# DeltaNet outputs produced channel-major by swapped matmul operands, with norms from VectorE block transposes

## The chip, the core and the metric

The kernel runs on one core of a Trainium2 chip. The metric is device microseconds of one execution. The engines are PE (TensorE, matmul and its weight loads), DVE (VectorE), ACT (ScalarE), POOL (GpSimd) and SP (SyncE, which here only issues DMAs). Each engine works through its own instructions in a fixed order, and an instruction that waits holds everything behind it on that engine.

## The reference

One hybrid layer: the normalised input goes through one projection; its columns feed three token mixers, DeltaNet (6 heads of 128), GLA (5) and forgetting attention (5); their outputs are gated, put side by side and go through one output projection. There are 512 tokens and 16 meta tokens ahead of them; the width is 2048. The part that the change touches is DeltaNet's output, its norm and its gate:

```python
def gated_head_norm(o, z, w):
    o = o * lax.rsqrt(jnp.mean(o * o, axis=-1, keepdims=True) + EPS) * w
    return o.reshape(z.shape) * jax.nn.silu(z)
...
    def step(s, inp):
        qk_c, qd, kd, u_c, w_c, gl = inp
        v_new = u_c - jnp.einsum('bhck,bhkv->bhcv', w_c, s)
        o = jnp.einsum('bhck,bhkv->bhcv', qd, s) + jnp.einsum('bhcs,bhsv->bhcv', qk_c, v_new)
        s = s * gl[..., None, None] + jnp.einsum('bhck,bhcv->bhkv', kd, v_new)
        return s, o
```

For each head and token the 128 channels of `o` are divided by their root mean square, multiplied by the channel's weight `w` and by the gate `silu(z)`. Queries are normalised to unit length first; the kernel folds that factor into the same norm.

## The kernel before

**The stream of weights.** Most of the time goes to the input and output projections. Each float32 weight block of 128x1024 is loaded (`raw`, by SP, L144), split into a rounded high part (`whi`, ACT, L167) and the rest (`wlo`, DVE, L168), and multiplied in three products with the split activations (`xh`, `xl`), in the matmuls of L242, into PSUM tiles `pp`. Evacuations (L363, L392) and the convolutions with SiLU (L612, L614 on DVE, L374 on POOL, L375 to L377 on ACT, L378 on DVE) follow each block. The mixers are put in between: their small matmuls stand between the big ones on PE, and their elementwise work between the splits on DVE, ACT and POOL. The program is written in the order of its parts; a scheduler that simulates a timeline then fixes each engine's order, with some places given by hand (`place`, `soon`, `late`, which name a position in the list of big matmuls). So an edit can move instructions that it doesn't name.

**DeltaNet** runs in two groups, g = 0 and 1, of three heads (H = 3). For each group `dn_keys` builds, over four blocks of 128 tokens and the meta block, the key transposes `pk` (PE, L679), decay tiles `e` (DVE L717, ACT L718, POOL L719), the scaled keys `kd` (L693), column factors `cols` (L704 to L709) and the products `an` (L723); `dn_values` transposes the values (`vp`); `dn_queries` the queries (`qT`); `dn_inverse` sends `an` through DRAM (the stores `scr`, the load `ab`, issued by ACT) and inverts its 32x32 blocks in a loop of 60 DVE instructions (L749, L753). The preparation of group 1 stands beside the mixing of group 0.

**`dn_mix`** goes over the four blocks b. Per block: `pks` and `py` (PE), `y` (ACT), the state step `psn`, the scores `pa` of the next block and its decayed queries `eg` (SP load from DRAM L924, ACT L925, POOL L928), and the output `po`: for each head two accumulating 128x128 matmuls (L971, L972). In `po` tokens lie on the partitions and channels along the row. ACT squares each head with a running sum (L975), four small instructions on DVE and ACT make the factor of each token, and ACT writes the scaled `on` (L984). One block later `gated` transposes `on` by PE (L902, tile `pt`) and DVE multiplies it with the channel weight `dnws` and the gate, in place in the gate's tile `zsdz` (L905), which is channel-major. After the group, SP stores the three `zsdz` to DRAM (`zd`, L1362).

**The query norms** (`query_sums`) take the sum of squares of `qT` over channels, which lie on partitions there: DVE transposes 32x32 blocks (L885), POOL squares (L888), DVE sums pieces (L889), and one matmul with the constant `fold` (L891) adds the pieces across partition quarters. `fold` is made from the identity by two DVE instructions (L832, L833) inside the tile `vpm`, in `dn_values`.

**Buffers.** Tag `t15` (128x384) has six buffers that all the three-head tiles share; `qs` (the workspace of the query norms) has one; PSUM tag `m` holds the mixers' PSUM tiles.

## Time and profile before

| what | value |
|---|---|
| time, median of 3 runs | 967.24 us (965.45 to 969.41) |
| the profiled execution | 966.72 us |
| its span, first to last instruction | 964.8 us |
| granted clock of TensorE, mean | 0.999 |
| busy: DVE, ACT, POOL | 688.2, 474.5, 233.0 us |
| output transposes L902 on PE | x24, 4.6 us busy |
| scalings L905 on DVE | x24, 6.9 us busy |
| squares L975 and scaled copies L984 on ACT | x24 each, 6.3 and 7.0 us busy |
| the blocks of group 0, group 1 | first `po` 251.8 us; last L905 477.3 us |

Read the span as PE's: all other engines have idle time, and what they do costs something only where PE waits for it. Matmul durations overlap, since matmuls are pipelined, so differences between starts tell the real price of one. The lines on which the prediction rests are shown in it.

### The profile page before, as it was taken

The numbers are of one execution on the slowest core, as the hardware profiler recorded it, in microseconds if no ns is written. First come the engines' busy times: TensorE is split into PE (matmuls) and PEld (weight loads), VectorE is DVE, ScalarE is ACT, GpSimd is POOL, SyncE is SP. The second block draws the span as 40 slices with busy tenths as digits, with TensorE's granted clock in tenths as the row PEclk, the third lists the DMA queues.
The fourth block names the chain that finished last, engine by engine and source line by source line (L and its number), as shares of the span: only waits on it lengthen the run. The fifth ranks groups of instructions, "written<-read, shape, count | busy, mean of one in ns | idle before, by whom it ended". The sixth has DMA issues, their size and how long they took to land.

```text
span 964.8 us, 18868 instructions
## 1 busy us (share of the span) xinstructions
PE 955.4 (99%) x7271; PEld 882.4 (91%) x7271; DVE 688.2 (71%) x1491; ACT 474.5 (49%) x1004; POOL 233.0 (24%) x262
## 2 busy tenths in 40 slices
...
GB/s 355 298 136 209 180 205 212 287 227 227 171 167 221 226 233 192 188 119 83 186 133 179 158 185 180 187 216 225 190 210 175 181 285 281 131 218 217 178 128 175
DMA packets 70334, 191.86 MB, mean 199 GB/s; under 512 B 14077, under 2 KB 17325, under 8 KB 69476
## 3 DMA queue, kind: packets, MB, share of 16 engines
...
q14 instruction: 33, 0.27, 0.1%
...
## 4 chain that ended last, share of the span: by engine, by line
PE 97%; DVE 1%; DMA 1%; ACT 0%; issue 0%; POOL 0%; ACTq 0%; SPq 0%; DVEq 0%; POOLq 0%
PE pp L242 48%; PE pp_a L569 8%; PE pq L1452 6%; PE pp L321 5%; PE pa L1452 3%; PE pt L1452 3%; PE ps L1452 3%; PE pp_b L569 2%; PE pp_c L569 2%; PE pp_d L569 2%; PE pr L1452 1%; PE pss L1087 1%; PE pfo L1328 1%; PE pfa L1279 1%; PE pgate L415 1%; PE pg L716 1%
## 5 line engine op out<-in xcount | busy, mean ns | idle before, releaser
L242 PE MATMUL pp<-xh,whi 128*128 128x264 f32 (+2 forms) x1120 | 269.6, 305 | 0.0
L242 PE MATMUL pp<-xl,whi 128*128 128x264 f32 (+2 forms) x1120 | 269.6, 305 | 0.0
L242 PE MATMUL pp<-xh,wlo 128*128 128x264 f32 (+2 forms) x1120 | 268.4, 305 | 0.2 <-DVE wlo L168 0.2
L167 ACT CAST whi<-raw 128x1024 fp32r<-128x1024 f32 x131 | 137.2, 1047 | 158.8 <-PE pp L242 97.3
L168 DVE TENSOR_TENSOR wlo<-raw,whi 128x1024 fp32r<-128x1024 f32 x131 | 165.0, 1260 | 62.6 <-ACT whi L167 59.9
L242 PEld LDWEIGHTS pp<-xh,whi 128*128 128x128 f32 x1120 | 181.2, 188 | 8.9 <-issue 0.3
L242 PEld LDWEIGHTS pp<-xl,whi 128*128 128x128 f32 x1120 | 181.5, 189 | 8.4
L242 PEld LDWEIGHTS pp<-xh,wlo 128*128 128x128 f32 x1120 | 181.1, 189 | 8.8 <-DVE wlo L168 0.5
L374 POOL TENSOR_SCALAR stc<-cv 128x528 f32<-128x528 f32 (+1 forms) x18 | 29.0, 1614 | 104.1 <-DVE cv L614 88.1
L614 DVE SCALAR_TENSOR_TENSOR cv<-pb,cpk,cv 128x528 f32<-128x528 f32 (+1 forms) x54 | 40.8, 756 | 0.6
L168 DVE TENSOR_TENSOR wlos<-raws,whis 128x1024 fp32r<-128x1024 f32 x20 | 24.2, 1222 | 14.6 <-ACT whis L167 14.6
L167 ACT CAST whis<-raws 128x1024 fp32r<-128x1024 f32 x20 | 20.7, 1049 | 26.8 <-PE pq L1452 12.5
L321 PE MATMUL pp<-xh,wf 128*128 128x512 f32 x128 | 33.1, 398 | 0.0
L1481 POOL TENSOR_TENSOR acc<-acc,fw 128x512 f32<-128x512 f32 x4 | 6.1, 1544 | 107.9 <-DVE wll L168 107.9
L569 PE MATMUL pp_a<-t,whi 128*128 128x264 f32 (+1 forms) x224 | 29.7, 282 | 0.0
L321 PEld LDWEIGHTS pp<-xh,wf 128*128 128x128 f32 x128 | 24.2, 190 | 5.6
L569 PE MATMUL pp_a<-xl,whi 128*128 128x264 f32 x112 | 28.5, 287 | 0.0
L569 PE MATMUL pp_a<-xh,whi 128*128 128x264 f32 x112 | 28.4, 286 | 0.0
L569 PEld LDWEIGHTS pp_a<-t,whi 128*128 128x128 f32 x224 | 27.8, 188 | 0.1
L363 DVE TENSOR_TENSOR pb<-pp,rstd 128x264 f32<-128x264 f32 (+1 forms) x36 | 13.8, 424 | 18.1 <-PE pp L242 18.0
L374 POOL TENSOR_SCALAR stdz<-zdz 128x512 f32<-128x512 f32 x6 | 11.2, 1874 | 62.5 <-DMA ti<-in_w_in 50.0
L481 POOL DMA_DIRECT2D tw<-tw x16 | 13.4, 835 | 51.7 <-DVE wlo L168 25.3
...
## 6 DMA issues: line engine op xcount, KB each, us to landing
raw<-in_w_in SPq DMA_DIRECT2D x103, 512.0 KB, 3.9
ti<-in_w_in SPq DMA_DIRECT2D x28, 512.0 KB, 5.2
raw<-ti SPq DMA_DIRECT2D x28, 512.0 KB, 3.5
tw<-in_w_dn SPq DMA_DIRECT2D x20, 512.0 KB, 5.3
raws<-tw SPq DMA_DIRECT2D x15, 512.0 KB, 4.0
ti<-in_w_in POOLq DMA_DIRECT2D x14, 512.0 KB, 6.3
ti<-ti POOLq DMA_DIRECT2D x14, 512.0 KB, 6.3
tw<-in_w_dn POOLq DMA_DIRECT2D x10, 512.0 KB, 6.6
```

What stands on the lines that cost most here:

```text
L167: pace[0] = A.copy(hi, raw).ins
L168: pace[1] = V.tensor_tensor(out=lo, in0=raw, in1=hi.bitcast(F32), op=ALU.subtract).ins
L242: mm = PE.matmul(p_[:, :nt], wt[:, j * m : (j + 1) * m], xx[k][:, t0 : t0 + nt], start=(k == 0 and wt is hi and xx is xh), stop=(k == KT - ...
L321: PE.matmul(begun[i][0][0][:, :S], wt[:, i * P : (i + 1) * P], xx[k][:, NM:T], start=k + n == 0, stop=k == KT - 1 and n == 2)
L363: V.tensor_tensor(out=o, in0=p_[rows], in1=rstd[rows, t0 : t0 + n], op=ALU.mult)
L374: maxes.append(G.tensor_scalar_max(t, src, LOW).ins)
L415: PE.matmul(pgate[a][:, :HT], wg[k // 8][:, k % 8, :], xx[k][:, a * HT : (a + 1) * HT], start=(k == 0 and xx is xh), stop=(k == KT - 1 and ...
L481: x = G.dma_start(out=out_[s], in_=in_[s], accum_op=ALU.add, max_dma_last_dim=2048)
L569: m = PE.matmul(p_[:, cols], wt[:, j * P : (j + 1) * P], xx[j][part_][:, cols], start=first and i == 0, stop=i == len(todo) - 1, skip_grou ...
L614: V.scalar_tensor_tensor(out=c, in0=pb[:, t0 + w : w + T], scalar=cwc[:, blk, w : w + 1], in1=c, op0=ALU.mult, op1=ALU.add)
L716: PE.matmul(pg[:r, j * r : (j + 1) * r], kT[:, j, ts], kT[:, j, ts], start=True, stop=True)
L1452: mm = PE.matmul(p_, o_[:, s], w_, start=(first and n == 0), stop=(last and n == 2), skip_group_check=True)
```

## The change

The two output matmuls of each head swap their operands: `y` and `sst` are now the loaded ones, `at` and `eg` stream, so `po` comes out with channels on partitions, as `zsdz` has them. The 24 transposes and the scalings behind them, the 24 squares, the four small factor instructions of each block and the 24 scaled copies go. Per block DVE now transposes the 32x32 blocks of `po` into `ot` (L989), multiplies `po` by the channel weight and the gate into `zsdz` (L991), ACT squares `ot` (L993) and DVE sums pieces of 32 (L994) into a part of the `qs` tile. After the last block of the group `normed` folds the pieces by one matmul (`pqo`, L903), makes the factor of all blocks at once (L908 to L911), transposes it (`pf`, L913), copies it to `ft` (L915), stores it to DRAM by four small DMAs (`fd`, L918), loads it back broadcast to all 128 partitions (`fb`, L921, 128x1536), and POOL multiplies the three `zsdz` by it (L923). `fb` has the tag `qs`, with its one buffer. `fold` is now made in the `qs` tile too (L881, L882), at the start of `query_sums`. The tile `vpm` is smaller.

```diff
--- before.py
+++ after.py
@@ -824,14 +824,10 @@
 
     def dn_values(g, st):
         vp = six.tile([P, NN, P], F32, tag="six", name=f"vp{g}")
-        vpm3 = t15(f"vpm{g}")
+        vpm3 = t15(f"vpm{g}", (P, 2, P))
         vpm = vpm3[:, 0]
         vms = vpm3[:, 1]
         G.memset(vms, 0.0)
-        fold = vpm3[:, 2].rearrange("p (i a) -> p i a", i=4)
-        V.reduce_sum(fold[:, 0], ident.rearrange("p (i a) -> p a i", a=32), axis=mybir.AxisListType.X)
-        V.tensor_copy(fold[:, 1:], fold[:, 0].unsqueeze(1).to_broadcast([P, 3, 32]))
-        st["fold"] = vpm3[:, 2]
         br = st["br"]
         brm = st["brm"]
         G.memset(brm, 0.0)
@@ -874,12 +870,17 @@
         sq_ = wk.tile([P, NB, H], F32, tag="sqq", name=f"sqq{g}")
         so_ = wk.tile([P, NB, H], F32, tag="soo", name=f"soo{g}")
         f_ = wk.tile([P, 2, NB, H], F32, tag="ff", name=f"ff{g}")
-        egs, egls, ons = {}, {}, {}
+        egs, egls = {}, {}
+        zt = triples["dz", g]
 
         def query_sums():
 
             qs = wk.tile([P, 2 * T + 2 * S], F32, tag="qs", bufs=1, name=f"qs{g}")
-            sums = qs[:, H * S : H * S + 16 * H].rearrange("p (h m) -> p h m", h=H)
+            sums, st["sums"], st["fold"] = (qs[:, H * S + a : H * S + b] for a, b in ((0, 16 * H), (16 * H, 32 * H), (32 * H, 32 * H + P)))
+            f4 = st["fold"].rearrange("p (i a) -> p i a", i=4)
+            V.reduce_sum(f4[:, 0], ident.rearrange("p (i a) -> p a i", a=32), axis=mybir.AxisListType.X)
+            V.tensor_copy(f4[:, 1:], f4[:, 0].unsqueeze(1).to_broadcast([P, 3, 32]))
+            sums = sums.rearrange("p (h m) -> p h m", h=H)
             for j in range(H):
                 t = qs[:, j * S : j * S + S]
                 x = V.transpose(t, qT[:, j, NM:])
@@ -896,14 +897,30 @@
             A.activation(f_[:, 0], sq_, AF.Ln, bias=eps_c)
             A.activation(f_[:, 1], f_[:, 0], AF.Exp, scale=-1.0)
 
-        def gated(b):
-            pt = psm.tile([P, 512], F32, tag="m", name=f"pt{g}{b}")
+        def normed():
+
+            pq = psm.tile([P, 512], F32, tag="m", name=f"pqo{g}")
+            PE.matmul(pq[:, : 16 * H], st["fold"], st["sums"], start=True, stop=True)
+            for i in range(4):
+                r = slice(32 * i, 32 * i + 32)
+                A.copy(so_[r], pq[r, : 16 * H].rearrange("p (b h i) -> p b h i", h=H, i=4)[:, :, :, i])
+            f1, f2 = f_[:, 0], f_[:, 1]
+            V.tensor_tensor(out=f2, in0=f2, in1=so_, op=ALU.mult)
+            A.activation(f2, f2, AF.Ln, scale=1.0 / (P * P), bias=eps_c)
+            V.tensor_tensor(out=f1, in0=f1, in1=f2, op=ALU.add)
+            A.activation(f1, f1, AF.Exp, scale=-0.5)
+            pf = psm.tile([P, 512], F32, tag="m", name=f"pf{g}")
+            PE.transpose(pf[: NB * H, :P], f1.rearrange("p b h -> p (b h)"), ident)
+            ft = t15(f"ft{g}", (NB * H, P))
+            A.copy(ft, pf[: NB * H, :P])
+            fd = drp.tile([H, NB, P], F32, name=f"fd{g}")
+            for b in range(NB):
+                nc.sync.dma_start(out=fd[:, b], in_=ft[b * H : b * H + H])
+            fb = wk.tile([P, 2 * T + 2 * S], F32, tag="qs", bufs=1, name=f"fb{g}")[:, : H * S]
+            fb = fb.rearrange("p (h t) -> p h t", h=H)
+            nc.sync.dma_start(out=fb, in_=fd.rearrange("h b t -> h (b t)").partition_broadcast(P))
             for j in range(H):
-                PE.transpose(pt[:, j * P : (j + 1) * P], ons[b][:, j, :], ident)
-            for j in range(H):
-                o = zs["dz", H * g + j][:, b * P : (b + 1) * P]
-                V.scalar_tensor_tensor(out=o, in0=pt[:, j * P : (j + 1) * P], scalar=dnws[:, 0:1], in1=o,
-                                       op0=ALU.mult, op1=ALU.mult)
+                G.tensor_tensor(out=zt[:, j, :S], in0=zt[:, j, :S], in1=fb[:, j], op=ALU.mult)
 
         def soon(mm, b, i):
             if g == 1:
@@ -963,29 +980,22 @@
                     V.scalar_tensor_tensor(out=sn[:, j, :], in0=sst[:, j, :], scalar=egl[:, j : j + 1],
                                            in1=pn[:, j * P : (j + 1) * P], op0=ALU.mult, op1=ALU.add)
                 scores(b + 1)
-            if b:
-                gated(b - 1)
             po = psm.tile([P, 512], F32, tag="m", name=f"po{g}{b}")
             for j in range(H):
                 pj = po[:, j * P : (j + 1) * P]
-                PE.matmul(pj, at[:, b * H + j, :], y[:, j, :], start=True, stop=False)
-                PE.matmul(pj, eg[:, j, :], sst[:, j, :], start=False, stop=True)
-            for j in range(H):
-                sq = wk.tile([P, P], BF16, tag="sq", name=f"sqo{g}{b}{j}")
-                A.activation(sq, po[:, j * P : (j + 1) * P], AF.Square, accum_out=so_[:, b, j : j + 1])
-
-            f1, f2 = f_[:, 0, b, :], f_[:, 1, b, :]
-            V.tensor_tensor(out=f2, in0=f2, in1=so_[:, b, :], op=ALU.mult)
-            A.activation(f2, f2, AF.Ln, scale=1.0 / (P * P), bias=eps_c)
-            V.tensor_tensor(out=f1, in0=f1, in1=f2, op=ALU.add)
-            A.activation(f1, f1, AF.Exp, scale=-0.5)
-            on = t15(f"on{g}{b}")
-            for j in range(H):
-                A.activation(on[:, j, :], po[:, j * P : (j + 1) * P], AF.Copy, scale=f1[:, j : j + 1])
-            ons[b] = on
+                PE.matmul(pj, y[:, j, :], at[:, b * H + j, :], start=True, stop=False)
+                PE.matmul(pj, sst[:, j, :], eg[:, j, :], start=False, stop=True)
+            ot = t15(f"ot{g}{b}")
+            V.transpose(ot.rearrange("p h t -> p (h t)"), po[:, : H * P])
+            zb = zt[:, :, b * P : (b + 1) * P]
+            V.scalar_tensor_tensor(out=zb, in0=po[:, : H * P].rearrange("p (h t) -> p h t", h=H), scalar=dnws[:, 0:1],
+                                   in1=zb, op0=ALU.mult, op1=ALU.mult)
+            A.activation(ot, ot, AF.Square)
+            V.reduce_sum(st["sums"][:, 4 * H * b : 4 * H * (b + 1)], ot.rearrange("p h (i c) -> p (h i) c", c=32),
+                         axis=mybir.AxisListType.X)
             if b < NB - 1:
                 sst = sn
-        gated(NB - 1)
+        normed()
 
 
     def tok_values(parts, name, v, t512, t16):
```

In the changed program line numbers lie 4 lower behind `dn_values` and 10 higher behind `dn_mix` (the stores `zd` are L1372).

**PE, the end of group 0.** In these rows `pp22_0` and `pp22_1` are the two halves of one projected block, `pt03` the last output transposes of group 0, `pk14`, `pk10`, `pk11` key transposes of group 1. Before (the last of three `pt03`, which alternate with `pk14`, and what follows):

```order
L902 MATMUL pt03_2492<-ident_79,on03_2488 128x128
L679 MATMUL pk14_3044<-ident_79,kT1_2647 16x128
L679 MATMUL pk10_3061<-ident_79,kT1_2647 128x128 x3
L679 MATMUL pk11_3079<-ident_79,kT1_2647 128x128 x3
L242 MATMUL pp22_1_3773<-xl5_241,whi22_0_3777 128x258
L242 MATMUL pp22_0_3772<-xh5_240,wlo22_0_3778 128x258
```

and now, around the first small matmuls behind group 0's last block:

```order
L242 MATMUL pp22_0_3730<-xl7_285,whi22_0_3735 128x258
L913 MATMUL pf0_2445<-ident_79,ff0_2242 12x128
L679 MATMUL pk14_3004<-ident_79,kT1_2607 16x128 x3
L679 MATMUL pk10_3021<-ident_79,kT1_2607 128x128 x3
L679 MATMUL pk11_3039<-ident_79,kT1_2607 128x128 x3
L242 MATMUL pp22_1_3731<-xl7_285,whi22_0_3735 128x258
```

The transposes `pt03` are gone, the factor's transpose `pf0` stands in their stead, 12 big matmuls (L242) further back, and the key transposes of group 1 have moved behind it.

**SP, the stores at the end of group 0.** `raw24_0` to `raw25_0` are weight blocks of the input projection, `tw` rows of a table copied by the way. Before:

```order
L144 DMA raw23_1_3957<-in_w_in 128x1024
L146 DMA tw_670<-in_w_dn 16x8192
L1362 DMA zd_671<-zsdz0_527 128x512 x3
L144 DMA raw24_0_4484<-in_w_in 128x1024
L146 DMA tw_670<-in_w_dn 16x8192
L144 DMA raw24_1_4515<-in_w_in 128x1024
```

and now:

```order
L144 DMA raw23_1_3915<-in_w_in 128x1024
L146 DMA tw_670<-in_w_dn 16x8192
L918 DMA fd0_2449<-ft0_2447 3x128 x4
L921 DMA fb0_2454<-fd0_2449 128x1536
L144 DMA raw24_0_4404<-in_w_in 128x1024
L146 DMA tw_670<-in_w_dn 16x8192
L1372 DMA zd_671<-zsdz0_527 128x512 x2
L144 DMA raw24_1_4435<-in_w_in 128x1024
L146 DMA tw_670<-in_w_dn 16x8192
L1372 DMA zd_671<-zsdz0_527 128x512
L144 DMA raw25_0_4477<-in_w_in 128x1024
```

The stores of the factor and its broadcast load stand ahead of `raw24_0`; the three stores of the outputs have moved behind `raw24_0` and are parted by `raw24_1`.

**DVE, the preparation of group 1.** `cv4` is a convolution, `cols1`, `an1` and `anm1` belong to `dn_keys` of group 1, `vpm1` and `qs1` are the tiles in which `fold` was and is made. Before, some dozen rows behind the last products of `cv4` (L614):

```order
L709 TENSOR_TENSOR cols1_3042<-cols1_3042 128x12
L709 TENSOR_TENSOR cols1_3042<-cols1_3042 16x3
L723 SCALAR_TENSOR_TENSOR anm1_3040<-pg14_3149,cols1_3042,e214_3150 16x16 x3
L723 SCALAR_TENSOR_TENSOR an1_3036<-pg10_3162,cols1_3042,e210_3163 128x128 x3
L723 SCALAR_TENSOR_TENSOR an1_3036<-pg11_3175,cols1_3042,e211_3176 128x128 x3
L723 SCALAR_TENSOR_TENSOR an1_3036<-pg12_3188,cols1_3042,e212_3189 128x128 x3
L832 TENSOR_REDUCE vpm1_3215<-ident_79 128x32
L839 COPY cols1_3042<-cols1_3042 16x1
L168 TENSOR_TENSOR wlo24_0_4488<-raw24_0_4484,whi24_0_4487 128x1024
L833 COPY vpm1_3215<-vpm1_3215 128x96
L723 SCALAR_TENSOR_TENSOR an1_3036<-pg13_3201,cols1_3042,e213_3202 128x128 x3
```

and now:

```order
L693 TENSOR_SCALAR kd1_2994<-pk12_3057,at1_2995 128x128 x3
L693 TENSOR_SCALAR kd1_2994<-pk13_3075,at1_2995 128x128 x3
L704 TENSOR_TENSOR cols1_3002<-cols1_3002 128x12
L704 TENSOR_TENSOR cols1_3002<-cols1_3002 16x3
L614 SCALAR_TENSOR_TENSOR cv4_3845<-pb4_3729,cpk_90,cv4_3845 128x512
L881 TENSOR_REDUCE qs1_4209<-ident_79 128x32
L705 SCALAR_TENSOR_TENSOR cols1_3002<-cols1_3002 128x12
L705 SCALAR_TENSOR_TENSOR cols1_3002<-cols1_3002 16x3
L614 SCALAR_TENSOR_TENSOR cv4_3845<-pb4_3729,cpk_90,cv4_3845 128x512
L882 COPY qs1_4209<-qs1_4209 128x96
L706 COPY cols1_3002<-cols1_3002 128x12
L706 COPY cols1_3002<-cols1_3002 16x3
```

The reduction that makes `fold` stood behind the third triple of products `an1`; now it stands ahead of the column factors (L705), between the last two products of `cv4`, with its copy three instructions further. Its tile is the next user of the one `qs` buffer after `fb0`, so it waits for the broadcast's landing and for the last of POOL's three products.

## The prediction

> **What bounds the kernel now.** I read the busy times first, then the chain of work that ended last, then the table of waits of PE, then the windows around the place where the change inserts new work.
>
> ```profile
> PE 955.4 (99%) x7271; PEld 882.4 (91%) x7271; DVE 688.2 (71%) x1491; ACT 474.5 (49%) x1004; POOL 233.0 (24%) x262
> ...
> PE 97%; DVE 1%; DMA 1%; ACT 0%; issue 0%; POOL 0%; ACTq 0%; SPq 0%; DVEq 0%; POOLq 0%
> ```
>
> ```profile
> PE warm L310 <- POOL ones L115: 1.2, 1, 1.2
> PE pp L242 <- DVE wlo L168: 0.2, 1, 0.2
> PE pp_b L569 <- ACT whi L167: 0.2, 1, 0.2
> ```
>
> PE is the bound all the way: it is busy for 99% of the span, the chain runs through it for 97%, and its three waits sum to 1.6 us, 1.2 of them at the start. Two rules follow. An instruction taken from PE is worth its issue spacing at once, wherever it stands. Work taken from DVE and ACT is worth nothing by itself, but a wait that is put on them can starve PE, whose weights they split (whi L167 on ACT, wlo L168 on DVE). So I ask where DVE has no room.
>
> ```profile
> 305.00:372.00 67.00, 67.00 (x379) 58.10 (x378) 58.54 (x148) 23.47 (x45) 23.20 (x24) 1.00 0.83 223
> 372.00:520.00 148.00, 148.00 (x1434) 139.65 (x1433) 84.63 (x195) 62.53 (x148) 35.94 (x42) 1.00 0.58 148
> ```
>
> In these rows the columns are length, PE, PEld, DVE, ACT, POOL busy, then clock, DMA share and GB/s. From 305 to 372 us DVE is busy 58.5 of 67 us (87%): this is where the second group's inverse is built, just behind the end of the first group. Behind the second group DVE is busy 84.6 of 148 us (57%). The first place is the one to fear.
>
> **PE: removed and added.**
>
> ```profile
> 266.79 0.49 PE L902 MATMUL pt<-ident,on 128*128 128x128 f32 x3
> 267.12 0.39 PE L971 MATMUL po<-y,at 128*128 128x128 f32 x2
> ```
>
> ```profile
> 247.41 0.32 PE L891 MATMUL pq<-qs,vpm 128*128 128x48 f32 x2
> 247.55 0.49 PE L242 MATMUL pp<-xh,wlo 128*128 128x264 f32 x2
> ```
>
> The durations overlap, so I take differences of starts. Three output transposes take 267.12 − 266.79 = 0.33 us, 0.11 each; 24 go: −2.64 us. Added per group are one 48-column fold matmul, at most 0.14 (247.55 − 247.41, there two with nothing between), and one transpose, 0.11: 2 × 0.25 = +0.50. Net −2.14 us, −1.07 for each group. The output matmuls swap which operand is loaded and which streams; count and shape stay. I cost that at 0: in the rows above one more 128x128 matmul adds 0.10 to 0.11 (0.49 for three, 0.39 for two) whether it is pt or po.
>
> **DVE and ACT inside the blocks.**
>
> ```profile
> L905 DVE SCALAR_TENSOR_TENSOR zsdz<-pt,dnws,zsdz x24: 329/343/351, 267.6 to 477.3; 128x128 f32<-128x128 f32 x24
> ...
> L922 DVE TENSOR_TENSOR at<-pa,at x8: 549/550/557, 241.6 to 454.6; 128x384 f32<-128x384 f32 x8
> ...
> L885 DVE STREAM_TRANSPOSE qs<-qT x6: 668/670/711, 215.2 to 386.5; 128x512 f32<-128x512 f32 x6
> ...
> L889 DVE TENSOR_REDUCE qs<-qs x6: 670/672/675, 218.3 to 392.1; 128x16 f32<-128x512 f32 x6
> ...
> L978 DVE TENSOR_TENSOR ff<-ff,soo x8: 158/164/564, 257.3 to 471.1; 128x3 f32<-128x3 f32 x8
> ...
> L925 ACT ACTIVATE eg<-eg x8: 508/524/530, 241.9 to 454.1; 128x384 f32<-128x384 f32 x8
> ```
>
> Per block DVE loses 3 × 0.343 + 2 × 0.164 = 1.36 us. It gains a block transpose of 384 elements, 0.67 × 384/512 = 0.50; a product of the size of L922, 0.55; a reduction of 384, 0.50: 1.55. That is +0.19 a block, 1.5 us in all, hidden behind PE as the 13% and 43% idle allow. ACT loses three squares with their accumulator reads, two small steps and three scaled copies a block and gains one square of the size of L925, 0.52: it is relieved. In place of the scalings, the gate product now waits only for `po`, not for the norm. Nothing of this is on PE's path, unless the block's next step stands behind it; the rivals price that.
>
> **The new chain at the end of a group.** In the changed order the factor's transpose pf0 comes 12 big matmuls past the old place of the last output transposes, with the key transposes L679 behind it.
>
> ```profile
> 300.87 0.37 PE L242 MATMUL pp<-xl,whi 128*128 128x258 f32 x1
> ...
> 302.29 0.40 PE L242 MATMUL pp<-xl,whi 128*128 128x258 f32 x2
> ```
>
> ```profile
> 301.36 1.30 SPq L1362 DMA_DIRECT2D zd<-zsdz  x3
> ```
>
> ```profile
> gb<-gd ACTq DMA_DIRECT2D x2, 792.0 KB, 6.2
> ...
> zd<-zsdz SPq DMA_DIRECT2D x6, 256.0 KB, 7.4
> ...
> fqk<-gd ACTq DMA_DIRECT2D x5, 264.0 KB, 3.7
> ...
> scmeta<-anm ACTq DMA_DIRECT2D x2, 3.0 KB, 2.0
> ```
>
> ```profile
> L1481 POOL TENSOR_TENSOR accs<-accs,fw x8: 1292/1310/1331, 939.7 to 948.4; 128x512 f32<-128x512 f32 x8
> ...
> L1111 POOL TENSOR_TENSOR gt<-gt,gqk x3: 1808/2458/3248, 490.6 to 599.4; 128x512 f32<-128x512 f32 x2, 64x512 f32<-64x512 f32 x1
> ```
>
> Twelve matmuls past 300.87 is 302.29; less the twelve small matmuls of that block that are now gone or behind (12 × 0.11 = 1.32) and nine earlier output transposes (0.99), plus the fold (0.14): pf0 at 300.1. With 0.27 for its passage (its spacing of 0.11 and the 0.16 by which a run of three, 0.49, outlasts its 0.33) and an ACT copy, put at 0.5 like L925's 384 elements, ft0 stands at 300.9. SP then issues four small stores fd; three issues took 1.30 us, so four take 1.7: 302.6. Their landing: 2.0 us (a 3 KB store, scmeta) to 7.4 (zd<-zsdz, the larger stores from the same place); I take 3, near the small one, as these move 1.5 KB each: 305.6. The broadcast fb (768 KB to 128 partitions) then lands 6.2 us after its issue, by gb<-gd of 792 KB in the same form; its own issue 0.4: 305.6 + 0.4 + 6.2 = 312.2; bounds 3.7 (fqk<-gd, a third of the bytes) and 7.4. Three POOL products of 128x512: 1.31 each alone, 2.46 where crowded. I take 1.35: POOL ends at **316.3**. All low ends together give 302.6 + 2.0 + 0.4 + 3.7 + 3.9 = 312.6, all high ends 325.2.
>
> Hidden or not?
>
> The outputs go to DRAM behind it and are read back only for the output projection, so they themselves have time. Three engines' queues carry the wait, though.
>
> ```profile
> 305.85 1.53 DVE L168 TENSOR_TENSOR wlo<-raw,whi 128x1024 fp32r<-128x1024 f32 x1
> ...
> 326.65 1.21 DVE L168 TENSOR_TENSOR wlo<-raw,whi 128x1024 fp32r<-128x1024 f32 x1
> ```
>
> ```profile
> 312.58 0.34 SPq L144 DMA_DIRECT2D raw<-in_w_in  x1
> ```
>
> ```profile
> raw<-in_w_in SPq DMA_DIRECT2D x103, 512.0 KB, 3.9
> ```
>
> SP: between raw24_0 and raw24_1 (312.58) now stand two of the stores zd<-zsdz, which need POOL's products; raw24_1 moves to about 315.2 and lands at 319, while its split wlo24_1 stood at 326.65: covered by 7 us. DVE, ACT and POOL: the decay tile e213 takes over the slot of ft0, so it waits for fd's landing (305.6); it stands behind wlo23_0 (305.85 to 307.4): covered by 1.8 us, and beyond that any excess waits ahead of the next place, not on top of it. The third is a buffer. The fold matrix, made on DVE in L832 of before in a tile of its own, is now made in the `qs` tile (L881), whose tag has one buffer, and fb uses the same tag. So **DVE waits at L881 of the second group until POOL's third product is done**, and all of DVE's work queues behind: the column operations L705 to L709, wlo, and the products `an` L723, which the store scr of ACT awaits.
>
> ```profile
> 313.96 0.23 DVE L705 SCALAR_TENSOR_TENSOR cols<-cols 128x12 f32<-128x12 f32 x2
> ...
> 320.64 0.86 DVE L723 SCALAR_TENSOR_TENSOR an<-pg,cols,e 128x128 f32<-128x128 f32 x3
> ...
> 307.31 2.41 DVE L693 TENSOR_SCALAR kd<-pk,at 128x128 f32<-128x128 f32 x9
> ```
>
> ```profile
> 333.50 0.20 DVE L749 TENSOR_TENSOR ab<-ab 51x30 f32<-51x30 f32 x1 [0.43 <-DMA ab<-scr]
> ...
> 337.17 0.69 DVE L378 TENSOR_TENSOR qT<-cv,stc 128x512 f32<-128x512 f32 x1 [1.51 <-ACT stc L377]
> ...
> 338.28 0.68 DVE L392 TENSOR_TENSOR zgz<-pp,rstd 128x512 f32<-128x512 f32 x1
> ...
> 345.42 1.21 DVE L168 TENSOR_TENSOR wlo<-raw,whi 128x1024 fp32r<-128x1024 f32 x1
> ...
> 356.73 1.21 DVE L168 TENSOR_TENSOR wlo<-raw,whi 128x1024 fp32r<-128x1024 f32 x1
> ```
>
> ```profile
> 347.91 0.40 PE L242 MATMUL pp<-xh,wlo 128*128 128x512 f32 x1
> ```
>
> ```profile
> 359.00 0.40 PE L242 MATMUL pp<-xh,wlo 128*128 128x512 f32 x1
> ```
>
> DVE would come to L881 at 313.96 plus six `kd` that now stand later (2.41/9 = 0.27 each, 1.6), less 0.4 for what the removed scalings free: about 315.2. It waits 316.3 − 315.2 = 1.1 us. From there to the last `an` stands the same work as from 313.96 to 321.50 before, 7.5 us: `an` ends at 323.8 instead of 321.5, so the inverse, which starts when scr and ab have gone through DRAM, starts 2.3 us later (1.2 without the wait). Up to the evacuation of zgz0 (338.28) one L614 of 0.66 moves in, while the qT product and the idle 1.51 ahead of it (2.1 together) move out: +0.85. From there the weight split of 345.42 (wlo26_0) ends at 346.63 and PE first uses it at 347.91 (its place in the order of PE's matmuls counted off): slack 1.28. PE now arrives 1.07 earlier, so the slack is 0.21, and the delay 0.85, or 1.45 if the qT product finds no idle time: a stall of 0.64 to 1.24. For the next but one (wlo27_0, from 356.73 to 357.94, used at 359.00, slack 1.06) it is 0.2 more. I take **1.2 us**; it grows one for one with the end of POOL, and it does not fall to nothing without the wait, but to some 0.2. Group 0 nets −1.07 + 1.2 = +0.1.
>
> Group 1: the same chain, but nobody reuses `qs` behind it, and DVE has the room shown above. PE loses 1.07. Two of GLA's score steps, 24 big matmuls apart before, now stand together; what prepares the later one had 24 × 0.12 = 2.9 us between them. Between 0 and 0.5 I charge 0.3: −0.8.
>
> **Sum:** 966.72 us of the profiled execution (964.8 span, 1.9 around it) + 0.1 − 0.8 = 966.0. The median of the runs shown is 0.5 higher, so on that footing **966.5 us**. A measurement of this kernel can tell about 0.5%, 4.8 us, from no change: this is no change.
>
> The Trainium skill (SBUF — State Buffer, "Who interferes with whom") says that a DVE instruction with two SBUF inputs and a GpSimd one that reads SBUF exclude each other for the whole instruction. L1481 beside L1111 (1.31 against 2.46 us for 128x512) agrees that neighbours matter. By it, POOL's products would be cheap in group 0 just because DVE waits at L881; were DVE still busy, the sum above would take the 2.46.
>
> **Rivals.**
>
> *No wait (A).* If fd takes 2.0 and fb 4.5 us (between the 3.7 and the 6.2), POOL ends at 302.6 + 2.0 + 0.4 + 4.5 + 4.0 = 313.5, ahead of DVE. The stall falls to 0.2, the sum to 966.72 − 2.14 + 0.2 + 0.3 = 965.1, 965.6 on the median. For it: fqk's 264 KB land in 3.7. Against it: gb's 6.2 is the nearest in size and form.
>
> The Trainium skill (DMA: Bandwidth & Descriptors, "Anatomy of one DMA — SWDGE (gpsimd) path") gives about 2.0 us fixed and 436 GB/s, an estimate of 3.8 us for 768 KB. By this rule rival A holds; gb<-gd at 6.2 speaks against it.
>
> *DVE held long (B, slower).* One mechanism: both DMAs in series land as late as zd<-zsdz does at this place, 7.4 each, and the products run at 2.46. POOL ends at 302.6 + 7.4 + 0.4 + 7.4 + 7.4 = 325.2, 8.9 later; the stall grows by as much: 966.5 + 8.9 = 975.4. It decides from POOL's end at 316.3 + 4.8 + 0.7 = 321.8 on. For it: DMA share 0.83 in this window, the highest. Against: fd is tiny, and DVE idles at the time.
>
> *The blocks pay (C).* The transposes are gone, but block transposes and reductions now stand in DVE's queue ahead of the state steps; if each block holds PE up for the added transpose, 0.50 × 8 = 4.0 us: 970.5.
>
> **How the numbers follow.** Forecast 0.58, A 0.20, B 0.14, C 0.08. The forecast's own range is 964.5 to 969. The range for 8 in 10 takes in A less the scatter of the runs (the lowest lies 1.8 below the median) and C with the near part of B: 963.8 to 971.2. Faster by over 0.5% needs 962.4, more than the whole saving on PE: 0.03. Slower by over 0.5% is most of B and a tail of C: 0.14. The same: 0.83.
>
> **What would show it.** PE's matmul starts: no L902, pqo and pf at 0.11 to 0.14. DVE idle ahead of L881 of group 1, released by POOL, about 1.1 us (A: none; B: over 6). PE waits on wlo near 345 to 360 us, about 1.2 (B: up to 10). fb's landing 6.2 after its issue, fd's 3. Block reductions at 0.5 with no PE wait on `py` or `psn` (C: 0.5 in each). The forecast is wrong if PE waits at another place, or if group 1 waits as well.

## The result and the profile after

| | before | after |
|---|---|---|
| median | 966.53 us, 6 runs (965.45 to 969.41) | 974.25 us, 4 runs (973.36 to 976.9) |
| profiled execution | 966.72 us | 976.9 us |
| its span | 964.8 us | 975.2 us |
| ratio after/before | | 1.0082, interval 1.0058 to 1.0105 |

The change is slower by 0.8%, 7.7 us; forecast was no change. Two further executions of the changed kernel, of 1566 and 2415 us, were disturbed and are left out. The profiled execution of after lies 2.6 us above the median of its four.

The page's busy times and its chain of work that ended last, after:

```profile
PE 957.5 (98%) x7253; PEld 882.7 (91%) x7253; DVE 698.3 (72%) x1479; ACT 464.6 (48%) x938; POOL 239.1 (25%) x268
...
PE 82%; DMA 5%; DVE 5%; issue 3%; ACT 2%; POOL 1%; ACTq 0%; SPq 0%; POOLq 0%; DVEq 0%
```

PE's table of waits, after (us in total, times, longest):

```profile
PE pss L1097 <- DVE kq L1077: 3.0, 3, 1.6
PE pp_a L569 <- ACT vf L584: 1.8, 1, 1.8
PE py L962 <- DVE zz L958: 1.4, 1, 1.4
PE warm L310 <- POOL ones L115: 1.2, 1, 1.2
PE pp L242 <- DVE wlo L168: 1.0, 2, 0.8
PE pp L242 <- ACT whi L167: 0.7, 1, 0.7
```

PE has fewer instructions, and waits at `pss`, `pp_a` and `py`, where it did not before, and longer for weight splits. The chain now leaves PE for 18% of the span (3% before), by way of DMAs and DVE.

**Where the time went.** The big matmuls of the input projections are the same 4728 in both kernels and in the same order, so the start of the n-th can be compared. The rows e1 to e16 are experiments of the next section; each row is one profiled execution. The table has, at some of these matmuls, how much later than in the kernel before it starts, in us, counted from the one at 257.6 us of before, within the first group's blocks but ahead of the places that differ. Such a number is what PE has lost up to there; small matmuls that moved across a column show up in it too. The saving alone would be -1.1 at 335 and 406 and -2.1 from 508 on.

| start in before, us | 335 | 406 | 481 | 503 | 508 | 541 | 560 | 625 | 740 |
|---|---|---|---|---|---|---|---|---|---|
| after | 1.2 | 3.3 | 0.9 | 0.3 | 6.3 | 6.5 | 6.5 | 8.4 | 10.0 |
| e1, no tail | 0.6 | 1.3 | -0.1 | -0.1 | -0.1 | 0.6 | -0.2 | 0.3 | 0.2 |
| e2, no products | 1.5 | 4.2 | 1.8 | 0.8 | 4.2 | 4.3 | 4.8 | 6.3 | 6.3 |
| e6, both tails late | -1.1 | -1.1 | -1.0 | -0.7 | -0.7 | -0.7 | -0.6 | 7.7 | 8.7 |
| e9, tails moved | -1.1 | -1.1 | -0.8 | -0.4 | -0.5 | 1.2 | 6.6 | 6.6 | 6.2 |
| e14, loads ahead | -1.0 | -0.4 | -0.1 | 0.3 | 0.3 | 1.0 | 3.8 | 4.5 | 4.5 |
| e15, first group only | -0.7 | -0.7 | 0.6 | 1.2 | 1.2 | 1.2 | 1.5 | 2.3 | 2.3 |
| e16, second group only | 0.0 | 0.8 | -1.7 | -2.4 | 3.6 | 3.9 | 3.6 | 5.0 | 5.0 |

After loses in three places: behind the first group (up to 406 us), at GLA's score steps (the small matmuls `pss`, 503 to 508), and in the first head of the forgetting attention (about 625 to 640).

**First group.** The timeline of SP and POOL, then of DVE, in after (start, length, engine and line, tiles, and in brackets the idle time ahead and what ended it):

```profile
302.61 1.24 SPq L918 DMA_DIRECT2D fd<-ft  x4
304.87 0.35 SPq L921 DMA_DIRECT2D fb<-fd  x1
311.93 4.55 POOL L923 TENSOR_TENSOR zsdz<-zsdz,fb 128x512 f32<-128x512 f32 x3 [1.99 <-DMA fb<-fd]
```

```profile
312.32 1.77 DVE L614 SCALAR_TENSOR_TENSOR cv<-pb,cpk,cv 128x512 f32<-128x512 f32 x1
...
315.57 1.01 DVE L704 TENSOR_TENSOR cols<-cols 128x12 f32<-128x12 f32 x2
316.51 0.73 DVE L614 SCALAR_TENSOR_TENSOR cv<-pb,cpk,cv 128x512 f32<-128x512 f32 x1
317.17 0.37 DVE L881 TENSOR_REDUCE qs<-ident 128x32 f32<-128x128 f32 x1
317.47 1.48 DVE L705 SCALAR_TENSOR_TENSOR cols<-cols 128x12 f32<-128x12 f32 x2
...
325.05 0.87 DVE L723 SCALAR_TENSOR_TENSOR an<-pg,cols,e 128x128 f32<-128x128 f32 x3
...
339.81 0.20 DVE L749 TENSOR_TENSOR ab<-ab 51x30 f32<-51x30 f32 x1 [4.13 <-DMA ab<-scr]
```

POOL ends at 316.48, where the forecast had it. But DVE doesn't wait at L881; it gets there with work in hand, and that work was longer: L614 took 1.77 us beside the products and 0.73 right behind them, the two rows L704 1.01 instead of 0.23. Without these 1.8 us DVE would have come to L881 at 315.4 us. Behind it the two column factors L705 take 1.48 us (0.23 before), beside three selections on POOL:

```profile
317.03 1.82 POOL L695 TENSOR_SCALAR_AFFINE_SELECT at<-at 128x384 f32<-128x384 f32 x3
```

The last `an` ends at 325.92 (321.50 before), and the inverse starts at 339.81 (333.50 before), 6.3 us late. Two stalls of PE follow at 344.06 and 345.55, 0.75 us each; with what surrounds them PE falls back by 2.1 (1.2 to 3.3 from 335 to 406). Ahead of that there is one in the blocks. The load of block 3's `eg` in before, then in after, and who used it:

```profile
281.23 0.39 SPq L924 DMA_DIRECT2D eg<-gd  x1
```

```profile
275.25 0.53 SPq L941 DMA_DIRECT2D eg<-gd  x1
```

```profile
283.71 0.52 ACT L942 ACTIVATE eg<-eg 128x384 f32<-128x384 f32 x1 [9.40 <-DMA eg<-gd]
```

```profile
285.55 0.75 PE L962 MATMUL py<-zz,uf 128*128 128x128 f32 x4 [1.36 <-DVE zz L958]
```

The scheduler issues this load 6 us earlier than before, and PE's `py` of the block stands 36 big matmuls earlier. But the load is used only 8.5 us after its issue (why it takes so long isn't shown; in e12, which has the same order on PE and DVE up to 470 us, it is used 6.9 us after its issue and PE doesn't wait for `py`). On ACT the square of `ot` is queued behind the exponential L942, on DVE a copy of `eg` and the reduction of `ot`, and only behind those `zz`, for which PE waits.

**Second group.** The timeline of before, then of after, DVE's first differences for GLA's scores:

```profile
480.76 0.89 DVE L1033 TENSOR_SCALAR gvt<-pgk,cpk 128x264 f32<-128x264 f32 x2
...
487.79 0.41 DVE L1060 TENSOR_TENSOR gvt<-gqk 128x256 f32<-128x256 f32 x1
...
488.80 0.41 DVE L1062 TENSOR_TENSOR gpr<-gqk 128x256 f32<-128x256 f32 x1
```

```profile
487.60 0.88 DVE L1043 TENSOR_SCALAR gvt<-pgk,cpk 128x264 f32<-128x264 f32 x2
...
493.66 1.33 DVE L1070 TENSOR_TENSOR gvt<-gqk 128x256 f32<-128x256 f32 x1
494.92 1.51 DVE L1072 TENSOR_TENSOR gvt<-gqk 128x256 f32<-128x256 f32 x1
496.35 1.52 DVE L1070 TENSOR_TENSOR gpr<-gqk 128x256 f32<-128x256 f32 x1
497.79 0.41 DVE L1072 TENSOR_TENSOR gpr<-gqk 128x256 f32<-128x256 f32 x1
```

POOL, and the score steps on PE, in after:

```profile
492.51 5.07 POOL L923 TENSOR_TENSOR zsdz<-zsdz,fb 128x512 f32<-128x512 f32 x3 [10.75 <-DMA fb<-fd]
```

```profile
506.45 1.37 PE L1097 MATMUL pss<-kq 64*64 64x64 f32 x64 [1.19 <-DVE kq L1077]
509.40 0.81 PE L1097 MATMUL pss<-kq 64*64 64x64 f32 x32 [1.58 <-DVE kq L1077]
```

Two things meet. In the order of PE the gate product `pgk`, with which the chain of DVE instructions for GLA's scores begins, has moved behind the factor's transpose `pf1`, 39 big matmuls later, so DVE starts 6.8 us later; score steps that stood ahead of big matmuls 2912, 2931, 2955 and 2979 now stand ahead of 2941, 2967, 2967 and 2979. And the products fall on DVE's first three differences: from the first to the fourth it is 4.1 us (493.66 to 497.79), 1.0 before (487.79 to 488.80). PE waits 3.0 us in all for `kq`.

**Forgetting attention.** PE's clock behind its 1.8 us wait, which ends at 632.99 (length, then PE, PEld, DVE, ACT and POOL busy, granted clock, DMA share, GB/s; two wider windows and one that fits the drop):

```profile
633.00:637.00 4.00, 4.00 (x23) 4.00 (x24) 3.21 (x7) 2.72 (x4) 0.87 (x1) 0.68 0.48 159
637.00:640.00 3.00, 3.00 (x22) 2.76 (x21) 0.07 (x2) 0.63 (x6) 0.00 (x0) 0.86 1.01 256
634.41:637.82 3.41, 3.41 (x18) 3.41 (x17) 1.80 (x3) 1.41 (x3) 0.87 (x1) 0.50 0.57 197
```

The granted clock is 0.50 for 3.41 us, and the 0.68 and 0.86 are means over that stretch and its surroundings. At half the clock 3.41 us do the work of 1.7, so about 1.7 us are lost there (an estimate). PE loses 1.9 us up to 625 of before (the wait) and 1.6 more behind it.

### The profile page after: what moved, and what is told of

It reads as the page before. It is cut to its first block, busy times and chain, and to the rows that moved or that the text cites. A ratio compares the mean times of both kernels' runs of the same rounds, so it can differ in the third digit from the quotient of the medians.

```text
span 975.2 us, 18780 instructions
## 1 busy us (share of the span) xinstructions
PE 957.5 (98%) x7253; PEld 882.7 (91%) x7253; DVE 698.3 (72%) x1479; ACT 464.6 (48%) x938; POOL 239.1 (25%) x268
## 4 chain that ended last, share of the span: by engine, by line
PE 82%; DMA 5%; DVE 5%; issue 3%; ACT 2%; POOL 1%; ACTq 0%; SPq 0%; POOLq 0%; DVEq 0%
PE pp L242 37%; PE pp_a L569 7%; PE pq L1462 6%; PE pp L321 5%; PE pa L1462 3%; PE pt L1462 3%; PE ps L1462 3%; PE pp_d L569 2%; PE pp_b L569 2%; PE pp_c L569 2%; PE pr L1462 1%; DMA eg<-gd 1%; DVE wlo L168 1%; DMA fqk<-gd 1%; DMA zd<-gqk 1%
## 5 line engine op out<-in xcount | busy, mean ns | idle before, releaser
L242 PE MATMUL pp<-xh,whi 128*128 128x264 f32 (+2 forms) x1120 | 270.6, 306 | 0.7 <-ACT whi L167 0.7
L242 PE MATMUL pp<-xh,wlo 128*128 128x264 f32 (+2 forms) x1120 | 269.1, 305 | 1.0 <-DVE wlo L168 1.0
L242 PE MATMUL pp<-xl,whi 128*128 128x264 f32 (+2 forms) x1120 | 269.1, 305 | 0.0
L242 PEld LDWEIGHTS pp<-xh,whi 128*128 128x128 f32 x1120 | 181.4, 188 | 10.1 <-ACT whi L167 1.2
L242 PEld LDWEIGHTS pp<-xh,wlo 128*128 128x128 f32 x1120 | 181.3, 189 | 10.2 <-DVE wlo L168 1.9
L242 PEld LDWEIGHTS pp<-xl,whi 128*128 128x128 f32 x1120 | 181.3, 189 | 8.2
L614 DVE SCALAR_TENSOR_TENSOR cv<-pb,cpk,cv 128x528 f32<-128x528 f32 (+1 forms) x54 | 41.9, 775 | 0.8
L375 ACT ACTIVATE stc<-stc 128x528 f32<-128x528 f32 (+1 forms) x18 | 11.5, 639 | 32.9 <-POOL stc L374 27.3
L945 POOL TENSOR_TENSOR eg<-eg,qT 128x384 f32<-128x384 f32 x8 | 8.1, 1012 | 77.7 <-DVE egl L944 54.0
```

Of the source, the lines that this page charges most:

```text
L242: mm = PE.matmul(p_[:, :nt], wt[:, j * m : (j + 1) * m], xx[k][:, t0 : t0 + nt], start=(k == 0 and wt is hi and xx is xh), stop=(k == KT - ...
L375: A.activation(t, t, AF.Exp, scale=-1.0)
L614: V.scalar_tensor_tensor(out=c, in0=pb[:, t0 + w : w + T], scalar=cwc[:, blk, w : w + 1], in1=c, op0=ALU.mult, op1=ALU.add)
L945: G.tensor_tensor(out=eg, in0=eg, in1=qT[:, :, ts], op=ALU.mult)
```

## The experiments

Times are medians; ratios are against the kernel before, with their intervals. "Tail" is what stands behind a group's last block: factor transpose, stores `fd`, broadcast `fb`, POOL's products, stores `zd`.

### e1 to e3: the tail and its products

e1 drops the whole tail, e2 only POOL's products, e3 doubles them:

```diff
-        normed()
```

```diff
-            for j in range(H):
-                G.tensor_tensor(out=zt[:, j, :S], in0=zt[:, j, :S], in1=fb[:, j], op=ALU.mult)
```

```diff
+                for _ in range(2):
+                    G.tensor_tensor(out=zt[:, j, :S], in0=zt[:, j, :S], in1=fb[:, j], op=ALU.mult)
```

> The outputs keep the swapped matmuls, block transposes, gate products and reductions, but the whole tail of each group is left out (fold matmul, factor, its store, the broadcast load, POOL's products), so the outputs aren't normalised. Both theories (lock: POOL's products and DVE's two-input instructions hold each other up; order: the tail stands ahead of the next section and pushes that section's first matmuls back) say that all but the blocks' own cost goes: 966.5 - 2.6 + about 1.4 (the one wait py <- zz seen in a block) = 965.3, between 964 and 967. If the blocks themselves pay, 968 or more.

> Only POOL's three products of each group are left out (the outputs aren't normalised); factor, stores and broadcast load stay, and PE's order at the end of group 1 is that of the change (pf1 at big matmul 2813, pgk at 2833, the first scores at 2941). Lock theory: the reductions and products of DVE beside them run at their usual 0.4 us, PE's waits on the score operands fall from 3.0 to under 1 us and those on the weight splits of group 0 go: 969 to 970. Order theory: the chain of the score operands still starts late, the waits stay near 3 us: 973 to 975.

> Each of POOL's products is done twice (the outputs are scaled twice). Lock theory: DVE loses another 3 us in each group; in group 1 the score operands come 3 us later, PE's waits there go from 3.0 to about 6, and in group 0 another 2 to 4 are lost: 978 to 981. Order theory: group 1 is unchanged (waits near 3.0), group 0 gains a wait at the fold: 974 to 977.

Measured: e1 967.19 us (0.9998, 0.9987 to 1.001), e2 972.84 us (1.0059, 1.0038 to 1.008), e3 980.94 us (1.0145, 1.0129 to 1.016). Without the tail nearly the whole loss is gone, but not the first group's: e1 is 1.3 us late at 406, where PE has more than 1 us less to do, and waits 1.0 for `py`. The second group's blocks give their saving in full (1.3 to -0.1 from 406 to 481).

Without the products the medians differ by 1.4 us only. In the second group e2 nets nothing (4.2 at 406, 4.2 at 508), where after nets 3.0: the products are worth 3.0 us there, and the later `pgk` alone takes back the saving. In the first group nothing comes back, and here DVE does stand waiting. But the edit also moved DVE's order: L881 now stands ahead of an evacuation (L363), a weight split, six `kd` and L704, which stand ahead of it in after, so DVE comes to it at 309.98 instead of 317.17:

```profile
313.04 0.38 DVE L881 TENSOR_REDUCE qs<-ident 128x32 f32<-128x128 f32 x1 [3.06 <-DMA fb<-fd]
```

The fold matrix waits 3.06 us for the broadcast into its tile, and the inverse starts at 339.61, as late as in after. So in the first group the tail costs DVE some 3 us in both orders: as a wait in e2, as 1.8 and 1.3 us of stretched work in after.

Doubled products add 6.7 us (980.94 - 974.25), the time that the lock theory gave. In the first group PE waits 4.3 us for the products `anm`, and not because of the fold, which stands behind them here: the column factors are held for as long as POOL's second three products and its selections run, to 322.6 us.

```profile
317.22 5.48 DVE L705 SCALAR_TENSOR_TENSOR cols<-cols 128x12 f32<-128x12 f32 x2
```

In the second group PE falls back by 6.2 us from 406 to 508, 3.2 more than in after, but the waits for `kq` fall to 1.4 us instead of rising to 6: PE waits 2.2 us for a weight split ahead of them, and 0.6 for ACT. And the granted clock is 0.50 for 3.41 us at the first wait and for 6.83 at the others. So part of the 6.7 us is not DVE's own delay.

### e7 and e8: what POOL's products do to DVE

Both are the kernel before with one addition: three POOL products of 128x512, or eight POOL memsets, on an unused tile, released when DVE begins GLA's differences.

```diff
+            for j in range(H):
+                z = zs["dz", H + j][:, :S]
+                G.tensor_tensor(out=probe[:, j * S : j * S + S], in0=z, in1=z, op=ALU.mult)
```

```diff
+            for j in range(8):
+                G.memset(probe[:, j % H * S : j % H * S + S], 0.0)
```

> The kernel before the change, plus three POOL products of 128x512 that read group 1's gated tiles and write an unused buffer, released by a three-column DVE copy just ahead of the first pair's score operands; the orders of PE, ACT and SP and the rest of DVE's are those of before. Lock theory: the six 256-element DVE differences and products beside them take 1.3 to 1.5 us in place of 0.41, the first scores' operands come some 3 us later, and PE waits 0.5 to 2 us at the scores: 967 to 969. Otherwise DVE's durations stay and so does the time, 966.5.

> The same probe, with eight POOL memsets of 128x512 (0.55 us each, about the time of the three products) in place of the products: POOL writes and reads nothing. If DVE is held by POOL's reads alone, its rows stay at 0.41 us and the time at 966.5. If any POOL work of that length holds it, the rows and the time are those of the probe with products.

The timelines of e7 (first two fences) and of e8 (last two):

```profile
486.89 3.50 POOL L1044 TENSOR_TENSOR probe<-zsdz 128x512 f32<-128x512 f32 x3 [9.70 <-DVE probe L1041]
```

```profile
486.71 0.42 DVE L1066 TENSOR_TENSOR gvt<-gqk 128x256 f32<-128x256 f32 x1
487.05 1.26 DVE L1068 TENSOR_TENSOR gvt<-gqk 128x256 f32<-128x256 f32 x1
488.24 1.26 DVE L1066 TENSOR_TENSOR gpr<-gqk 128x256 f32<-128x256 f32 x1
489.42 1.26 DVE L1068 TENSOR_TENSOR gpr<-gqk 128x256 f32<-128x256 f32 x1
```

```profile
488.30 3.79 POOL L1043 MEMSET probe<- 128x512 f32 x8 [9.67 <-DVE probe L1041]
```

```profile
488.49 0.42 DVE L1067 TENSOR_TENSOR gvt<-gqk 128x256 f32<-128x256 f32 x1
488.82 0.42 DVE L1065 TENSOR_TENSOR gpr<-gqk 128x256 f32<-128x256 f32 x1
489.15 0.42 DVE L1067 TENSOR_TENSOR gpr<-gqk 128x256 f32<-128x256 f32 x1
```

One DVE difference with two inputs lasts as long as one POOL product (3.50/3 = 1.17) plus a little, three times in a row; beside memsets none is longer. e7 took 968.02 us (1.0015, 1.0006 to 1.0025), e8 966.76 us (1.0004, 0.9995 to 1.0013). So products that read, not POOL's work as such, hold DVE. With the old order PE is 1.1 to 1.6 us late behind it; 3 in after, where `pgk` comes late and leaves no slack. The Trainium skill (SBUF — State Buffer, "Who interferes with whom") says just this: a DVE instruction with two SBUF inputs contends with a GpSimd instruction that reads SBUF, not with one that only writes it. These runs agree, with 1.26 us beside the products and 0.42 beside the memsets.

### e5: `py` of block 3 later

```diff
-        "py01": (('dv', 5), 1),
+        "py01": (('dv', 5), 1), "py03": (('dv', 5), 133),
```

> The changed kernel with one more place given by hand: group 0's last py matmuls stand 15 big matmuls later (1766 instead of 1751; before the change 1787). If the block's loss is only that PE was put there too early, the wait of py on zz (1.4 us in the changed kernel) goes and the rest stays: 974.3 - 1.4 = 973. If the lateness is carried on through DVE, other waits grow by the same and the time stays at 974.

976.23 us (1.0102, 1.0087 to 1.0117), above both theories' numbers, though its interval meets that of after. The wait for `py` is gone, but PE then waits 2.4 us for `anm` and 0.9 for the sums, and is 4.6 us late at 406: with the tail where it is, the lateness is only handed on.

### e4, e6, e9, e12: the tail moved

In all four a group's tail is taken out of `dn_mix` and called later; of the first group ahead of the second's mixing, of the second behind GLA's first pair (e4), or behind the score steps of the second (e6) or first pair (e9). e6 and e9 have `py03` of e5 too. e12 moves only the second group's, as e9. From the edit of e9 (the second half of the test on `g` is always true):

```diff
-        normed()
+        st["f1"] = normed()
+        def out():
+            tail()
+            for h in range(H * g, H * g + H):
+                nc.sync.dma_start(out=zd[h], in_=zs["dz", h])
+        return out
...
+        if p == 0:
+            tails[1]()
         dd = t[:, :S]
...
-        dn_mix(g, st)
-        for h in range(H * g, H * g + H):
-            nc.sync.dma_start(out=zd[h], in_=zs["dz", h])
+        if g == 1 and 'mix' == "mix":
+            tails[0]()
+        tails.append(dn_mix(g, st))
...
```

> The same work, written later: of the tail only the fold matmul and the factor stay at the group's end; the factor's transpose, stores, broadcast load, products and the stores of the outputs of group 0 are written ahead of group 1's mixing, those of group 1 behind the first GLA pair. PE's order then has the first scores at 2912, 2931 and 2955 as before the change. Order theory: the saving on PE shows, 966.5 - 2.1 + about 1 = 965 to 966. Lock theory: the products meet DVE at another place; where it is not short of time they cost nothing, else up to 3 us in each group: 965 to 971.

> As in the run with the late tail, with py03 15 big matmuls later and the tail of group 1 written behind the scores of the second GLA pair, so that its products fall at about 570 to 585 us, where DVE was busy 9.8 of 20 us before the change. Order and lock theories together: no wait is left that the tail causes; the saving on PE shows, 966.5 - 2.1 + 0 to 0.5 = 964.4 to 965. If the wait in the first head of forgetting attention (3.5 us with its lowered clock in the changed kernel) has a cause of its own, 967 to 968.

> Change: the first group's tail (factor transpose, stores, broadcast, POOL's products) is moved behind the second group's mixing, the second group's tail right behind the score steps of GLA's first head pair, whose steps then keep their old places on PE; py03 stays where it was before the change. In the kernel with both tails moved later still, PE kept the whole saving to 573 us and lost it at FoX's tile; here the products fall at about 515 to 526 us, where DVE is busy 53% of the time and no score operands are made. Theory 1 (the loss is the tail's place: products beside DVE work that is due, and steps put behind the tail): PE waits fall to about 3 us, most of them at the forgetting attention's pp_a (1 to 2): 965.5 to 967.5. Theory 2 (the blocks themselves cost PE, wherever the tail stands): 970 or more, with waits on py, pqo and pg in group 0's blocks. Theory 3 (the broadcast in the one-buffer tile collides with whatever follows): DVE waits for POOL at fqkp again, 971 to 975.

> Change: the changed kernel, with only the second group's tail moved, behind the score steps of GLA's first pair; the first group as in the change. Theory 1 (the second group lost 5 us net of its 1.07: 3 from the key steps that stand behind the factor's transpose, 3 from products beside the score operands): about 4 to 5 us below the changed kernel, 969.5 to 970.5; PE waits on kq gone. Theory 2 (group 0's lateness is what shows up there): 973 to 975, and PE waits elsewhere. What is left over the kernel before is then group 0 (3.3 us by the trace) plus the forgetting attention.

| | time | ratio, interval | where PE loses |
|---|---|---|---|
| e4 | 971.80 us | 1.0051 (1.0036 to 1.0066) | 3.0 at the second pair's scores, 1.8 in the forgetting attention |
| e6 | 975.24 us | 1.0091 (1.0074 to 1.0108) | 8.3 between 560 and 625 |
| e9 | 972.64 us | 1.0065 (1.0053 to 1.0077) | 7.1 between 508 and 560, at the second pair's scores |
| e12 | 974.54 us | 1.0084 (1.0071 to 1.0097) | 7.9 between 508 and 560 |

In e6 and e9 PE is 1.1 us ahead at 406 us: with the tail away and `py` of block 3 15 big matmuls later (ahead of 1766; 1787 before, 1751 in after), the first group pays what was counted. In e12 the first group is as in after, yet by the same comparison only 1.0 us late at 406, without the wait for `py`; e10 below, with after's orders, is 2.6 late. So after's 3.3 is the value of one execution. The second group's 1.1 does not appear at 481 in e6 and e9: the first group's tail now stands beside its mixing, and PE waits 0.6 to 0.9 us for a weight split there. In e12 `pgk` is back (ahead of 2788) and so are the score steps, and nothing is lost up to 508. But a larger loss moves along with the second tail. e4 and e6 came out above every number that was expected, and in e9 and e12 the times that fit are those of the theories that blame something else than the tail's place, though not by their mechanisms (DVE waits for no POOL product at the forgetting attention in e9; e16 below shows that the second group needs no lateness of the first). In e6 DVE stands at the evacuation of the forgetting attention's queries and keys, and right behind it 6.08 us more for the load `xb`, which POOL issues behind the products (at 572.77):

```profile
574.67 0.77 DVE L363 TENSOR_TENSOR fqk<-pp,rstd 128x264 f32<-128x264 f32 x2 [2.98 <-DMA zd<-zsdz]
```

What makes the rest of e6's loss wasn't traced. In e9 the products run alone, 3.74 us for three, and what stands behind them in the queues comes late. Timelines of SP and POOL, before and then e9:

```profile
515.40 1.22 SPq L1180 DMA_DIRECT2D gvt<-zd  x2
```

```profile
512.90 0.57 POOL L522 DMA_DIRECT2D xa<-in_xT  x1 [1.06 <-PE pgn L1145]
```

```profile
519.62 3.74 POOL L929 TENSOR_TENSOR zsdz<-zsdz,fb 128x512 f32<-128x512 f32 x3 [7.86 <-DMA fb<-fd]
523.31 0.60 POOL L522 DMA_DIRECT2D xa<-in_xT  x1
```

```profile
522.14 2.17 SPq L1008 DMA_DIRECT2D zd<-zsdz  x2
524.36 0.97 SPq L1203 DMA_DIRECT2D gvt<-zd  x2
```

While POOL waits 7.86 us for the broadcast, the load `xa` that it has to issue waits with it (523.31 instead of 512.90), and on SP the gate loads `gvt` stand behind the products' stores (524.36 instead of 515.40). Both feed DVE's work ahead of the second pair's scores.

### e13, e14: the queues behind the tail

e13 is e9 with the second group's stores `zd` behind the loads `gvt` on SP. In e14 they stand behind GLA's own stores as well, and on POOL the products behind the load `xa`.

```diff
+    for x, n in after_:
+        tc.add_manual_dep(x, issued_[n].name, mybir.DependencyInfo(
+            mybir.DependencyClass.NoSync, mybir.DependencyReason.DATA), reason="behind")
```

> Change: as the kernel with both tails moved (the second behind GLA's first pair's scores), but on SP the second group's stores zd stand behind the two loads gvt of GLA's gates instead of ahead of them; POOL's queue is left, with its load xa behind the products. In the kernel without this edit, gvt was issued at 524.36 us instead of 515.40, what it feeds (gqk, its store zd, the load fqk on ACT's queue at 543.18 instead of 534.54, the split whi behind that load) came 8 to 9 us late, and PE lost 7 us at 541 to 556 us. Theory 1 (the stores in SP's line carry the wait for POOL to GLA's next pair): gvt back at about 515 us, the load fqk at 535 to 538, the waits on kq there under 1 us, 966 to 968. Theory 2 (POOL's line, with xa behind the products, is what makes it late): DVE's input differences stay late, 970 to 972. Theory 3 (neither; the products and the blocks cost it): 972 to 973 as without the edit.

> Change: as the kernel with both tails moved, but with nothing that others need behind the wait for the broadcast: on POOL the load xa of the fifth chunk stands ahead of the products, on SP the second group's stores stand behind GLA's gate loads and the stores of its first pair's outputs. Theory 1 (orders behind the wait were the rest of the loss): PE keeps its 2.1 us, less up to 1 us at the second pair and up to 1 in the forgetting attention: 964.5 to 966.5, at or under the kernel before. Theory 2 (products and blocks cost it): 970 or more.

e13: 972.41 us (1.0061, 1.0047 to 1.0075), as without the edit (theory 3's number); its gate loads are issued at 518.46, still 3 us late, and POOL's line is as in e9. e14: 970.42 us (1.0039, 1.0027 to 1.0052): the loss between 508 and 560 is halved, 3.5 instead of e9's 7.1, and PE's waits for `kq` fall from 3.1 to 1.8. So the queues behind the wait were about half of it. Of the 3.5 that are left, 1.8 are the waits for `kq`, and 1.7 fit the granted clock, 0.50 for 3.41 us right behind them. That the time still lies where theory 2 put it doesn't show its mechanism; what still delays `kq` wasn't found.

### e10, e11: the forgetting attention's wait

ACT's copy `vf`, for which PE waits 1.8 us, stands behind two scalings of the input chunks `xe` that wait for their DMAs, 2.98 and 1.05 us (2.35 and none before). e10 lets the last two scalings come one weight split later; e11 does the same to e9.

```diff
-                waits.append((x.ins, len(heads_) + 2, heads_))
+                waits.append((x.ins, len(heads_) + 3, heads_))
```

> Change: the changed kernel, with the ACT scaling of the last two input chunks (xe, L544) due one weight split later, so that the copy vf L584, for which PE waits 1.8 us at 633 us, no longer stands behind two ACT operations that wait for xe's DMA. Theory 1 (ACT's waits for xe's landing, 2.98 and 1.05 us against 2.35 before, are what delays vf and with it PE): the wait pp_a <- vf falls under 0.3 us and the time by about 1.5 to 2.5 us, to 972 to 973. Theory 2 (the wait only moves, because xl is then late for PE): 974 to 975, with a wait of PE on xl or on another vf. Theory 3 (the wait is inherited from work behind schedule since the first group): PE waits elsewhere for as long, 974 or more.

> Change: the two edits together, the tails moved and xe's scaling one split later. Theory 1 (two separate causes): 1 to 2 us below the kernel with the tails alone, 964.3 to 966, under the kernel before by up to 2 us, since PE has 2.1 us less to do. Theory 2 (one cause, and the wait for xe was only a sign of it): the same time as with the tails alone, within 0.5 us.

e10: 973.11 us (1.0069, 1.0052 to 1.0087), PE's wait for `vf` 0.4 instead of 1.8. The scalings ahead of it did delay `vf`; by the time, 1.1 us less than after, that is within the intervals of the two. e11: 973.17 us (1.0066, 1.0054 to 1.0078), as e9, which had no such wait. Why the `xe` loads land later (up to 6.6 us, 5.1 before) isn't settled: e8, which has only the memsets, waits 0.8 us there, e1 0.3.

### e15, e16: each group alone

In e15 only the first group is made in the new way, its tail and `py03` moved as in e9; in e16 only the second, all as in the change. From e15's edit:

```diff
+            if g == 0:
                 for j in range(H):
                     pj = po[:, j * P : (j + 1) * P]
                     PE.matmul(pj, y[:, j, :], at[:, b * H + j, :], start=True, stop=False)
...
+            else:
                 for j in range(H):
                     pj = po[:, j * P : (j + 1) * P]
                     PE.matmul(pj, at[:, b * H + j, :], y[:, j, :], start=True, stop=False)
```

> Change: the first group's outputs are made as in the change, with its tail behind the second group's mixing; the second group's outputs are made as before. Theory 1 (the blocks save PE what was counted, and only what stands behind the tail took it back): PE keeps its 1.1 us to the end, 965.0 to 966.2, within the measurement of the kernel before but not above it. Theory 2 (any shift of PE's work against the fixed places further down costs more than the saving): 967 to 970, with waits behind 480 us where nothing of the second group was changed.

> Change: the second group's outputs and tail as in the change, the first group's as before. Theory 1 (the second group by itself loses about 5 us at GLA's score steps, 506 to 511 us, against a saving of 1.1): 970 to 972, waits of PE on kq of about 3 us. Theory 2 (most of that was handed down from the first group's lateness): 966.5 to 968, waits on kq under 1 us. The forgetting attention's wait for vf then shows whether it follows the second group (present, 1 to 2 us) or the first (absent).

e16: 971.24 us (1.0049, 1.0037 to 1.0061), by theory 1, with the same wait in PE's table:

```profile
PE pss L1145 <- DVE kq L1125: 3.0, 3, 1.6
```

PE goes from 0.8 us late at 406 to 3.6 late at 508: the second group loses 2.9 us net by itself, 4.0 against its saving, as in after (3.0 and 4.1), and nothing of it is handed down. (The step from 503 to 508 is 6 us, but score steps that moved across 503 are in it.) It costs 5.0 us by the medians (971.24 - 966.21), which leaves 3.0 of the change's 974.25 for the first group and for what the two do to each other. The wait for `vf` is there too, 1.2 us, so it doesn't need the first group either. e15: 967.31 us (1.0014, 1.0005 to 1.0023): 0.7 ahead at 406, then 1.3 lost up to 481, beside the second group's mixing, 0.6 up to 503, and 0.8 in the forgetting attention. That is theory 2: the saving is there and doesn't last. None of these kernels beats the one before.

## Why the prediction was wrong

**What held.** PE's saving: 1.07 us a group were counted, and e6 and e9 are 1.07 ahead at 406 us. The swapped operands cost nothing that shows. POOL's end, 316.48 (316.3), though by terms that cancel: the issues of `fd` ended 1.3 us later than forecast, its landing took 1.0 us from there instead of 3, the broadcast 7.1 from its issue instead of 6.6 (rival A had 4.5 for it, the estimate beside it 3.8), and the products 4.55 instead of 4.05. The place of the stall: PE waits ahead of 344.06 and of 345.55 us, once for ACT's part of a weight split and once for DVE's. Rivals A and B are out, since POOL ended on time; that B's 975.4 lies near the result is chance. Both of the signs that the prediction named for being wrong came: PE waits at other places (`py`, `pp_a`), and the second group waits as well.

**First group, forecast +0.1, measured +3.3 at 406 us.** Two sizes were off. The blocks were costed at nothing beside PE (rival C had 0.5 for each block); what came was a single wait at block 3, 1.4 us, by an `eg` load issued earlier but used 8.5 us after its issue and a `py` set earlier, with 2.3 us lost in all by 335 us (1.2 instead of -1.1; in e12, without that wait, 0.6). The prediction followed the new order only at the places of its sum, not for the block's own steps. And the stall was 2.1, not 1.2: the step that failed is "waits 1.1 us at L881". DVE's arrival there was sized rightly (315.2; 315.4 without the stretching), but it was still at work when the products began, and they held it up until 317.17, 0.9 us beyond the forecast's 316.3. Beside POOL's selections L705 then took 1.3 us longer, which stood in no term. So the last `an` came 4.4 us late instead of 2.3, the way of `scr` and `ab` through DRAM took 13.9 us instead of 12.0 (why isn't shown), and the inverse came 6.3 late. I wrote that the products would be cheap because DVE waits; the trace has the opposite case, which the prediction names in a condition ("were DVE still busy") but priced in no term of its sum.

**Second group, forecast -0.8, measured +3.0.** This is the step that decided the sign. I saw two score steps stand together and charged 0.3 us, since DVE had room (57% busy). Mean room says nothing here: DVE's chain from `pgk` to the first score operands is serial. It started 6.8 us later, because `pgk` had moved behind `pf1`, and the products stretched it by 3.1. Of the 4.1 us lost against the saving, the order makes 1.1 (e2) and the products 3.0 (after less e2), each from one execution; the second group alone shows the same loss (e16), and with its tail moved away nothing is lost there (e12). The products' price had been put in the first group only.

**The forgetting attention, forecast nothing, 3.5 in the profiled execution.** 1.8 are a wait, the rest lies where the clock is halved for 3.41 us. It was in no rival. This execution is 2.6 us slower than the median, so some of what it lost isn't typical; which part isn't shown. The path, ACT's scalings ahead of `vf`, is shown (e10); its first cause is open.
